# Feed forward accumulators over eight PSUM banks, and the modulation's sums over partitions later in the order

## The chip, the cores and the metric

One core of a Trainium2 chip runs the whole program. Its engines work side by side, each through its own list of instructions in a fixed order: TensorE (PE in the profile, with PEld for its weight loads), VectorE (DVE), ScalarE (ACT), GpSimd (POOL) and SyncE (SP), which here issues all DMAs. The metric is device time in microseconds of one execution. Matrix products accumulate in PSUM, which has eight banks; a tile of 128 x 512 f32 fills one bank.

## The reference, cut to what matters

Two transformer blocks on 1024 tokens of width 1024, all in f32. The part that the change touches is the feed forward at the end of the first block, and the modulation that opens the second:

```
u = causal_dwconv(h @ w_up, conv_w) + conv_b        # 1024 -> 2 x 2816 columns, 3 taps along the tokens
a, b = split(u, 2)
y = (silu(a) * b) @ w_down                           # 2816 -> 1024
h = h + rmsnorm(y, g5)

mod = silu(c) @ w_ada + b_ada                        # one row of 1024 times 1024 x 3072
shift, scale, gate = split(mod, 3)
h2 = rms_norm(h, g) * (1 + scale) + shift            # opens block 2; gate multiplies its output
```

## The kernel before, in words

The tokens are worked in two halves of 512. Each f32 operand is split into a high and a low part, so that one product is three matrix instructions (`mm3`, L178 to L180): high times high, high times low, low times high. A k tile of 128 rows of a weight comes as half of a 512 KB load into `raw`, is cut by ACT (high part `whi`, L143) and POOL (low part `wlo`, L144), and is used for four PSUM tiles, 12 instructions in all. `whi` and `wlo` have six buffers each, `raw` two.

PSUM's eight banks are divided by name. `A()` (L102) hands out tiles `pa` from four banks. `M()` (L105) hands out tiles `pm`: two banks without a name `ns`, and one bank each for `ns` 0 and 1. All large products of the feed forward use `A()`; transposes, the attention's small products and the modulation use `M()`.

`ffn` (L807) runs once per half, called FFN1 and FFN2 below. Its inner width of 2816 is 22 tiles of 128, in six groups: five of four tiles, and one of two. For one group, `up` (L814) makes two products of four PSUM tiles each, called up1 and up2 (96 instructions each; the last group has up1 alone). ACT copies each PSUM tile to `pad` (L817), DVE does the three taps of the convolution (L818 to L824), ACT the silu, DVE the product of the two halves (L829), and ACT and DVE split the result into `gh` and `gl`. Then `proj_R` makes the two halves of the output columns from the group before, called R0 and R1 (48 instructions each, 24 in the last group), and DVE adds each of their four PSUM tiles to `y` (L845 copies in the first group, L847 adds later). The order within the program is up1, up2, R0, R1 for each group. Since all four use the same four banks, each product begins when the readers of the one before have emptied them.

At the start of each `ffn` the other half of the tokens is still being normed. After `next(f)` has written up1 and up2 of the first group, `resid` adds the residual (L285 to L291) and `norm_T` (L294) norms the rows and transposes them over `pm` tiles (L223, eight tiles of four transposes) into the operand of the next stage, splitting each by ACT and DVE (L143, L144). The scheduler orders instructions by priority, so that this work of DVE stands between the convolutions of the first group. These two stretches, 1020 to 1080 us and 1440 to 1500 us, are called opening 1 and opening 2.

`mod` (L852) makes shift, scale and gate (j = 0, 1, 2). For each j, DVE multiplies eight blocks of `w_ada` by the column of silu(c) and adds them up in `mac` (L864, L866); each block is a 512 KB load into `wad`, of which there are two buffers. Then two products with a tile of ones sum `mac` over the partitions into `pm` tiles (L872, two passes each in the profile), DVE adds the bias (L873), and the row goes to DRAM (`mods`, L877), from where FFN2's opening reads scale and shift. `mod` is called in the opening of FFN1 with `high_priority(offset=-800)`, which lets its instructions be ordered later than their place in the code.

Of the kernel before, what the change touches and what calls it, by code (L numbers as in the profile page):

```python
# [9 lines left out]
F32 = mybir.dt.float32  # L10
# [7 lines left out]
P = 128  # L18
T = 1024
D = 1024  # L20
HT = 512
# [40 lines left out]
def weave(main, f, rate):  # L62
    """`rate` steps of f after each of main, then the rest of f"""
    due = 0.0
    for _ in main:
        due += rate
        while due >= 1:
            due -= 1
            next(f, None)
    run(f)  # L70


class Net:
    def __init__(self, tc, a, out):
        self.tc = tc
        self.nc = tc.nc
        self.a = a
        self.out = out

# [27 lines left out]

    def t(self, n, ns=""):
        return self.tp.tile([P, n], F32, name="tn", tag=f"tn{n}{ns}", bufs=8)
# [36 lines left out]
    # weights: src [pairs of k tiles, 128, 2, columns]  # L146
# [14 lines left out]
    def wplan(self, specs):  # L161
        """the units that wpair() hands out, in order"""
        self.wq = [src[i : i + 1] for src in specs for i in range(src.shape[0])]
        self.wready = []

    def wpair(self):
        """the next two k tiles, with the loads and splits of the following pairs under way"""
        while self.wq and len(self.wready) < LOOK:
            self.wready.append(self.wunits(self.wq.pop(0)))
        return self.wready.pop(0)  # L170
# [11 lines left out]
    # out[c, t]: 4 column tiles of 128, free = t  # L182
    def proj_T(self, units, xh, xl, nt=HT, ncol=4):
        ps = [self.A() for _ in range(ncol)]
        n = len(units)
        for k, (wh, wl) in enumerate(units):
            for c in range(ncol):
                s = slice(c * P, (c + 1) * P)
                self.mm3(ps[c][:, :nt], wh[:, s], wl[:, s], xh[:, k, :nt], xl[:, k, :nt], k == 0, k == n - 1)
        return ps  # L190

    # out[t, c]: t tiles of 128, free = columns
    def proj_R(self, units, xh, xl, ntt=NTT, nc=HT):
        ps = [self.A() for _ in range(ntt)]
        n = len(units)
        for k, (wh, wl) in enumerate(units):
            for t in range(ntt):
                s = slice(t * P, (t + 1) * P)
                self.mm3(ps[t][:, :nc], xh[:, k, s], xl[:, k, s], wh[:, :nc], wl[:, :nc], k == 0, k == n - 1)
        return ps  # L200
# [15 lines left out]
    # rows r [128, 1024] at t tile -> x hi/lo  # L216
# [12 lines left out]
    # rms norm of rows, times g, to x hi/lo  # L229
# [49 lines left out]
    def postnorm(self, y, g, hsrc, hdst):  # L279
        """y: two tiles [P, 4, 512]; y = hsrc + rms(y) g, also to hdst"""  # L280
        nc = self.nc
        r = self.sumsq_panels(y)
        for t in range(NTT):
            hr = self.R()
            nc.sync.dma_start(hr, hsrc[t * P : (t + 1) * P, :])  # L285
            for p in range(2):
                c = slice(p * HT, (p + 1) * HT)
                yt = y[p][:, t, :]
                nc.vector.scalar_tensor_tensor(yt, yt, r[:, t : t + 1], g[:, c], ALU.mult, ALU.mult)
                nc.vector.tensor_tensor(yt, yt, hr[:, c], ALU.add)  # L290
                nc.sync.dma_start(hdst[t * P : (t + 1) * P, c], yt)  # L291

    def norm_T(self, y, g, shift=None):
        """rms-normed rows of y (two panels), transposed"""  # L294
        nc = self.nc
        xh, xl = self.X(), self.X()
        r = self.sumsq_panels(y)
        for t in range(NTT):
            hr = self.R()
            for p in range(2):  # L300
                c = slice(p * HT, (p + 1) * HT)
                nc.vector.scalar_tensor_tensor(hr[:, c], y[p][:, t, :], r[:, t : t + 1], g[:, c], ALU.mult, ALU.mult)
                if shift is not None:
                    nc.vector.tensor_tensor(hr[:, c], hr[:, c], shift[:, c], ALU.add)
            self.rows_to_T([hr[:, :HT], hr[:, HT:]], xh, xl, t)
        return xh, xl
# [52 lines left out]
    def s1_qkv(self, u, xh, xl, qk, vv, gate):  # L359
        """q, k, v of the heads 2u, 2u + 1 after the short convolution, [d, t], and their gates, rows"""  # L360
# [22 lines left out]
        # the heads 0 and 1 bring the eight logits along  # L383
# [31 lines left out]
    def s1_specs(self):  # L415
        """the weights of stage 1 in the order of their use"""
        a = self.a
        first = [a["w_qk"][0], a["w_vga"][0], a["w_cfm"][0], a["w_qk"][1], a["w_vg"][0], a["w_cfm"][1]]
        second = [first[i] for i in (0, 1, 2, 5, 3, 4)]
        return first + second + 2 * [a["w_out"][0], a["w_out"][1]]  # L420

    def s1_ab(self, ab):
        """log decay and beta, [t, chunk, head]"""
# [37 lines left out]
    def s1_conv(self, j, xh, xl, cc):  # L461
        """gated and convolved conformer channels, [c, t]"""
# [52 lines left out]
    def gdn(self, u, qkv, dec, gate):  # L515
        """heads 2u, 2u + 1, 4 chunks of 128; multiplies the normed rows into `gate`"""
# [19 lines left out]
        # squares of q and k, summed over d  # L536
# [18 lines left out]
        def chunk(c):  # L555
# [19 lines left out]
            # decays  # L575
# [10 lines left out]
            # scores  # L586
# [8 lines left out]
            # (I + L)^-1 by doubling; U = -L^T, Xm the inverse within blocks, Y its transpose  # L595
# [30 lines left out]
            # the off-diagonal block of the two halves  # L626
# [18 lines left out]
            # scan  # L645
# [55 lines left out]
    # y = x @ w (rows), then the norms around the residual  # L701
# [41 lines left out]
    def xa_q(self, p, q, xh, xl):  # L743
        """queries of the heads 2p, 2p + 1"""
        units = self.wunits(self.a["xa_w_q"][p])
        ps = [self.A() for _ in range(4)]
        for k, (wh, wl) in enumerate(units):
            for c in range(4):
                s = slice(c * P, (c + 1) * P)
                self.mm3(ps[c], wh[:, s], wl[:, s], xh[:, k, :], xl[:, k, :], k == 0, k == NK - 1)  # L750
                yield
        for c in range(4):
            self.split(ps[c], q[0][:, 4 * p + c, :], q[1][:, 4 * p + c, :])
# [47 lines left out]
    def ffn(self, xh, xl, p3, fh):  # L801
# [6 lines left out]
        def up(kt, ng):  # L808
            gh = self.E(F32R)
            gl = p3.tile([P, 4, HT], F32R, name="gl", tag="gl", bufs=2)  # L810
            for j in range(0, ng, 2):
                ps = self.proj_T(self.wunits(wu[(kt + j) // 2]), xh, xl)
# [23 lines left out]
        for n, (kt, ng) in enumerate(groups):  # L836
# [3 lines left out]
            for p in range(2):  # L840
                units = self.wunits(wd[p, kt // 2 : (kt + ng) // 2])
                ps = self.proj_R(units, *g)
                for t in range(NTT):
                    if kt == 0:
                        v.tensor_copy(y[p][:, t, :], ps[t])  # L845
                    else:
                        v.tensor_tensor(y[p][:, t, :], y[p][:, t, :], ps[t], ALU.add)  # L847
# [4 lines left out]
    def mod(self, pm2):  # L852
# [5 lines left out]
        for j in range(3):  # L858
            ac = pm2.tile([P, D], F32, name="mac", tag="mac", bufs=1)
            for k in range(8):  # L860
# [4 lines left out]
                else:  # L865
                    v.scalar_tensor_tensor(ac, w, sc[:, k : k + 1], ac, ALU.mult, ALU.add)  # L866
            r = pm2.tile([P, D], F32, name="wad", tag="wad", bufs=2)
# [9 lines left out]
            nc.sync.dma_start(self.mods[j], r)  # L877

    def b2_open(self, ctx):
# [13 lines left out]
        # lower bounds  # L893
# [12 lines left out]
        # f = lb + (1 - lb) (tanh + 1) / 2  # L906
# [14 lines left out]
    def hgrn_head(self, i, qs, fe, vr, oA, ss):  # L921
        """qs, fe: silu(q) and tanh(f / 2), [d, t]; vr: [t, 4 tiles, 512] rows; head i"""
# [12 lines left out]
        # the two diagonal blocks of 64  # L935
# [43 lines left out]
        # rows of kG  # L979
# [6 lines left out]
        # states before the chunks 1..3 and after the last  # L986
# [21 lines left out]
    def gate_rows(self, zu, gu, xh, xl, gb, o, r):  # L1008
        """o [P, 4, 512] *= rstd[t, head] * silu(z) * sigmoid(g) * norm_g"""
# [16 lines left out]
    def rot(self, units, xh, xl, h, which):  # L1026
        """rows of 8 heads x 64, rotated, times the decay of the row -> [P, 4, 512]"""
# [21 lines left out]
    def ret_pair(self, i, qr, kr, vr, oB, ss):  # L1049
        """heads 2i, 2i+1"""  # L1050
# [159 lines left out]
    def final_proj(self, h, m, gate, fg):  # L1210
        """output projection and the final norm, row tile after row tile"""
# [36 lines left out]
    def run(self):  # L1248
# [3 lines left out]
        with ExitStack() as ctx:  # L1252
# [80 lines left out]
            with ExitStack() as c3:  # L1333
# [6 lines left out]
                xf = self.norm_T(y, gb(4))  # L1340
                with self.tc.high_priority(offset=-800):
                    self.mod(p3)
                *_, y = f
                f = self.ffn(*xf, p3, fh)
                next(f)
                self.resid(0, y, 2, 5)
                xb = self.norm_T(y, self.gbc(self.mods[1]), self.gbc(self.mods[0]))
                *_, y = f
            with ExitStack() as c4:
# [19 lines left out]
    def resid(self, h, y, s, gi):  # L1369
        """h_s = h_(s-1) + rms(y) g"""  # L1370
# [3 lines left out]
    def load_norm(self, src, g, ntt=NTT, shift=None, xs=None):  # L1374
        """rms-normed rows of src, transposed"""
# [8 lines left out]
def _host(inp):  # L1384
    """layout of the inputs and constants of the shapes"""
# [7 lines left out]
    # weights, a unit of columns after the other: [unit, pair of k tiles, 128, 2, columns]  # L1393
# [71 lines left out]
```

## Time and profile before

| what | value |
|---|---|
| median of 3 runs | 3004.94 us (3001.94 to 3011.28) |
| profiled execution, first to last instruction (its span) | 3007.8 us |
| TensorE busy in the profile | 2823.5 us, 94% |
| VectorE, GpSimd, ScalarE busy | 60%, 41%, 38% |
| feed forward, both halves | 1000.7 to 1823.8 us |

The profile gives no time of the profiled execution other than its span; it lies 2.9 us above the median of the timed runs. A matrix instruction is shown from its start to its modelled end, so that neighbours overlap: the pace is read from the distance of the starts. PEclk is the share of full clock that TensorE was granted; it has two levels, 1.0 (2.4 GHz) and 0.5 (1.2 GHz), and a fraction is a mean over a stretch.

### The profile page before, as it was taken

How to read it: one execution, taken by the hardware profiler on the slowest of the kernel's cores; microseconds unless marked ns; L12 is line 12 of the kernel's file. 1: busy time of each engine (PE TensorE's matmuls, PEld its weight loads, DVE VectorE, ACT ScalarE, POOL GpSimd, SP SyncE). 2: the span in 40 equal slices, each digit the busy share in tenths (PEclk: the TensorE clock that was granted, in tenths of full speed). 3: DMA queues.
4: the chain of work that ended last, by engine and by line, in shares of the span. 5: the costliest groups of instructions: out<-in, count | busy, mean ns of one | idle time of the engine just before them, and what ended most of it. 6: DMA issues, size and time to landing. Idle time of an engine off the chain costs nothing.

```text
span 3007.8 us, 41965 instructions
## 1 busy us (share of the span) xinstructions
PE 2823.5 (94%) x15828; PEld 2232.1 (74%) x15828; DVE 1813.9 (60%) x3605; ACT 1135.2 (38%) x2273; POOL 1234.5 (41%) x913
## 2 busy tenths in 40 slices
PE   7999898998999999899899999999999999999998
PEld 6676676777877777677677777787777777777776
DVE  6698889866345765743855556737545366464444
ACT  4443534455444433233433333232233333232333
POOL 3333323333342554354454544343443543434443
PEclk9999999999999999999999999999999999999999
DMA  4112111146242633622422225121323332222222
GB/s 152 50 64 64 50 45 55 36 133 192 68 140 86 202 99 100 208 91 84 130 91 91 85 91 170 51 88 56 96 74 97 99 119 71 82 63 83 85 75 101
DMA packets 136715, 287.07 MB, mean 95 GB/s; under 512 B 9792, under 2 KB 12736, under 8 KB 136512
## 3 DMA queue, kind: packets, MB, share of 16 engines
q1 hardware_dynamic: 136512, 284.38, 29.3%
q8 instruction: 125, 2.05, 0.3%
q14 instruction: 78, 0.64, 0.1%
HBM read 265.99 MB, written 18.35 MB: 95 GB/s over the span
## 4 chain that ended last, share of the span: by engine, by line
PE 49%; DVE 14%; ACT 2%; issue 2%; DMA 2%; POOL 1%; SPq 0%; ACTq 0%; DVEq 0%; POOLq 0%
PE pa L178 15%; PE pa L179 14%; PE pa L180 14%; DVE fo L824 3%; PE pm L944 2%; DVE fo L822 1%; POOL wlo L144 1%; DMA wad<-in_w_ada 1%; DVE fo L829 1%; DVE fh L819 1%; DVE pad L818 1%; DVE gl L144 1%; PE pm L1001 0%; PE pm L990 0%; PE pm L1000 0%
## 5 line engine op out<-in xcount | busy, mean ns | idle before, releaser
L144 POOL TENSOR_TENSOR wlo<-raw,whi 128x512 fp32r<-128x512 f32 (+1 forms) x792 | 1137.7, 1442 | 1668.7 <-ACT whi L143 1590.6
L143 ACT CAST whi<-raw 128x512 fp32r<-128x512 f32 (+1 forms) x808 | 496.7, 620 | 1131.3 <-PE pa L180 603.8
L178 PE MATMUL pa<-x,whi 128*128 128x512 f32 x1376 | 567.4, 413 | 18.8 <-ACT x L1130 10.3
L178 PE MATMUL pa<-whi,x 128*128 128x512 f32 (+2 forms) x1408 | 555.3, 396 | 12.4 <-ACT z L1015 3.8
L180 PE MATMUL pa<-x,wlo 128*128 128x512 f32 x1376 | 552.1, 401 | 0.1
L179 PE MATMUL pa<-x,whi 128*128 128x512 f32 x1376 | 551.9, 401 | 0.0
L180 PE MATMUL pa<-whi,x 128*128 128x512 f32 (+2 forms) x1408 | 547.5, 389 | 0.0
L179 PE MATMUL pa<-wlo,x 128*128 128x512 f32 (+2 forms) x1408 | 546.4, 388 | 0.0
L178 PEld LDWEIGHTS pa<-x,whi 128*128 128x128 f32 x1376 | 261.7, 190 | 82.1 <-ACT x L1130 11.2
L178 PEld LDWEIGHTS pa<-whi,x 128*128 128x128 f32 x1408 | 265.5, 189 | 75.6 <-issue 6.3
L180 PEld LDWEIGHTS pa<-x,wlo 128*128 128x128 f32 x1376 | 261.7, 190 | 62.5 <-issue 2.7
L180 PEld LDWEIGHTS pa<-whi,x 128*128 128x128 f32 x1408 | 265.5, 189 | 54.0 <-issue 0.9
L179 PEld LDWEIGHTS pa<-wlo,x 128*128 128x128 f32 x1408 | 265.6, 189 | 52.4 <-issue 1.2
L179 PEld LDWEIGHTS pa<-x,whi 128*128 128x128 f32 x1376 | 262.1, 190 | 54.2 <-issue 3.4
L480 DVE SCALAR_TENSOR_TENSOR e<-padc,cw,e 128x512 f32<-128x512 f32 x240 | 197.3, 852 | 1.2
L824 DVE SCALAR_TENSOR_TENSOR fo<-pad,cols,fo 128x512 f32<-128x512 f32 x176 | 168.5, 985 | 0.7
L178 PE MATMUL pa<-whi,e 128*128 128x512 f32 x352 | 143.3, 407 | 25.8 <-DVE e L847 20.4
L819 DVE COPY fh<-pad 128x2 f32<-128x2 f32 x88 | 27.3, 310 | 196.4 <-ACT pad L817 196.4
L179 PE MATMUL pa<-wlo,e 128*128 128x512 f32 x352 | 142.2, 404 | 0.0
L180 PE MATMUL pa<-whi,gl 128*128 128x512 f32 x352 | 141.9, 403 | 0.0
L144 DVE TENSOR_TENSOR x<-pm,x 128x512 fp32r<-128x512 f32 x112 | 75.0, 685 | 67.8 <-ACT x L143 67.3
L178 PEld LDWEIGHTS pa<-whi,e 128*128 128x128 f32 x352 | 68.0, 193 | 46.7 <-DVE e L847 23.9
(354 smaller groups left out, 3848.7 us busy)
## 6 DMA issues: line engine op xcount, KB each, us to landing
raw<-in_w_in SPq DMA_DIRECT2D x112, 512.0 KB, 3.7
raw<-in_ffn_w_up SPq DMA_DIRECT2D x88, 512.0 KB, 3.8
raw<-in_ffn_w_down SPq DMA_DIRECT2D x44, 512.0 KB, 4.0
raw<-in_w_out SPq DMA_DIRECT2D x32, 512.0 KB, 3.9
raw<-in_w_qf SPq DMA_DIRECT2D x32, 512.0 KB, 3.7
h<-e SPq DMA_DIRECT2D x48, 256.0 KB, 3.0
r<-h SPq DMA_DIRECT2D x24, 512.0 KB, 4.5
wad<-in_w_ada SPq DMA_DIRECT2D x24, 512.0 KB, 4.4
```

What stands on the lines that cost most here:

```text
L143: self.nc.scalar.copy(hi, src)
L144: (lo_eng or self.nc.vector).tensor_tensor(lo, src, hi.bitcast(F32), ALU.subtract)
L178: mm(ps, lhsT=lh, rhs=rh, start=first, stop=False)
L179: mm(ps, lhsT=lh, rhs=rl, start=False, stop=False)
L180: mm(ps, lhsT=ll, rhs=rh, start=False, stop=last)
L480: v.scalar_tensor_tensor(o, pad[:, k : k + HT], w(k), o, ALU.mult, ALU.add)
L818: v.tensor_copy(pad[:, :2], fh[:, i, :])
L819: v.tensor_copy(fh[:, i, :], pad[:, HT:])
L822: v.tensor_scalar(o, pad[:, 2:], self.col(k0 + 2), self.col(FB0 + i), ALU.mult, ALU.add)
L824: v.scalar_tensor_tensor(o, pad[:, k : k + HT], self.col(k0 + k), o, ALU.mult, ALU.add)
L829: v.tensor_tensor(ua, ua, ub, ALU.mult)
L944: mm(pm[64 * e : 64 * e + 64, c, :], lhsT=kG[:, s], rhs=q[:, s], start=True, stop=True)
```

## The change

A new function `banks` hands out four tiles of `A()` and four tiles of `M()` in turn, and the feed forward takes its accumulators from it. FFN1 calls it 23 times, so that FFN2's first product has the `pm` tiles. `mod` becomes a generator of four pieces: the sums of j = 0 and 1 in FFN1's opening, their products over the partitions and biases after FFN1, the sum of j = 2 in FFN2's opening, and its products after FFN2. `mac` gets a second buffer. The rest of the diff takes comments out, which moves line numbers (L178 to L180 are L184 to L186 in the changed kernel, L223 is L229, L866 is L873, L872 is L882).

```diff
+        self.turn = False
...
+    def banks(self):
+        self.turn = not self.turn
+        return [self.A() for _ in range(4)] if self.turn else [self.M(), self.M(), self.M(ns=0), self.M(ns=1)]
...
-    def proj_T(self, units, xh, xl, nt=HT, ncol=4):
-        ps = [self.A() for _ in range(ncol)]
+    def proj_T(self, units, xh, xl, nt=HT, ncol=4, ps=None):
+        ps = ps or [self.A() for _ in range(ncol)]
...
-                ps = self.proj_T(self.wunits(wu[(kt + j) // 2]), xh, xl)
+                ps = self.proj_T(self.wunits(wu[(kt + j) // 2]), xh, xl, ps=self.banks())
...
-                ps = self.proj_R(units, *g)
+                ps = self.proj_R(units, *g, ps=self.banks())
...
-        for j in range(3):
-            ac = pm2.tile([P, D], F32, name="mac", tag="mac", bufs=1)
+        def sums(j):
+            ac = pm2.tile([P, D], F32, name="mac", tag="mac", bufs=2)
...
+            return ac
+
+        def over_partitions(j, ac):
             r = pm2.tile([P, D], F32, name="wad", tag="wad", bufs=2)
...
+        acs = sums(0), sums(1)
+        yield
+        for j, ac in enumerate(acs):
+            over_partitions(j, ac)
+        yield
+        ac = sums(2)
+        yield
+        over_partitions(2, ac)
...
+                mod = self.mod(p3)
                 with self.tc.high_priority(offset=-800):
-                    self.mod(p3)
+                    next(mod)
                 *_, y = f
+                next(mod)
                 f = self.ffn(*xf, p3, fh)
                 next(f)
+                with self.tc.high_priority(offset=-800):
+                    next(mod)
                 self.resid(0, y, 2, 5)
                 xb = self.norm_T(y, self.gbc(self.mods[1]), self.gbc(self.mods[0]))
                 *_, y = f
+                run(mod)
```

On TensorE, between R0 and R1 of FFN1's first group, the last instructions of R0's fourth tile and the first of R1 stand so before:

```order
L178 MATMUL pa_10525<-whi_10518,e8_9495 128x512
L179 MATMUL pa_10525<-wlo_10519,e8_9495 128x512
L180 MATMUL pa_10525<-whi_10518,gl_9496 128x512
L178 MATMUL pa_10598<-whi_10580,e8_9495 128x512
L179 MATMUL pa_10598<-wlo_10581,e8_9495 128x512
L180 MATMUL pa_10598<-whi_10580,gl_9496 128x512
```

and so in the changed kernel:

```order
L184 MATMUL pa_10470<-whi_10463,e8_9495 128x512
L185 MATMUL pa_10470<-wlo_10464,e8_9495 128x512
L186 MATMUL pa_10470<-whi_10463,gl_9496 128x512
L184 MATMUL pm_10543<-whi_10525,e8_9495 128x512
L185 MATMUL pm_10543<-wlo_10526,e8_9495 128x512
L186 MATMUL pm_10543<-whi_10525,gl_9496 128x512
```

The order is the same; R1 now writes `pm` tiles while R0's `pa` tiles are being read.

On VectorE, in opening 1, before, the last sum of j = 0 (`mac`), and then the start of the residual's norm (`tn` are tiny columns of the reciprocal square root):

```order
L866 SCALAR_TENSOR_TENSOR mac_10033<-wad_10055,sc_10031,mac_10033 128x1024
L276 TENSOR_TENSOR tn_9876<-tn_9859 128x4
L136 TENSOR_SCALAR tn_9878<-tn_9876 128x4
L126 TENSOR_SCALAR tn_9881<-tn_9878 128x4
L127 TENSOR_SCALAR tn_9880<-tn_9881 128x4
L129 TENSOR_TENSOR tn_9881<-tn_9880 128x4
L130 SCALAR_TENSOR_TENSOR tn_9881<-tn_9881,tn_9878 128x4
```

In the changed kernel the same place reads:

```order
L873 SCALAR_TENSOR_TENSOR mac_10033<-wad_10055,sc_10031,mac_10033 128x1024
L871 TENSOR_SCALAR mac_10058<-wad_10059,sc_10031 128x1024
L873 SCALAR_TENSOR_TENSOR mac_10058<-wad_10062,sc_10031,mac_10058 128x1024
L873 SCALAR_TENSOR_TENSOR mac_10058<-wad_10065,sc_10031,mac_10058 128x1024
L282 TENSOR_TENSOR tn_9876<-tn_9859 128x4
L142 TENSOR_SCALAR tn_9878<-tn_9876 128x4
L132 TENSOR_SCALAR tn_9881<-tn_9878 128x4
L133 TENSOR_SCALAR tn_9880<-tn_9881 128x4
L135 TENSOR_TENSOR tn_9881<-tn_9880 128x4
L873 SCALAR_TENSOR_TENSOR mac_10058<-wad_10068,sc_10031,mac_10058 128x1024
L136 SCALAR_TENSOR_TENSOR tn_9881<-tn_9881,tn_9878 128x4
```

Sums of j = 1 (`mac_10058`) have come in front of the norm and into it: three of the eight in front, two within the reciprocal square root, two behind the residual, one in front of the second norm.

On TensorE, in opening 2, before, the third and the fourth group of transposes (`pm_13108`, `pm_13115`) stand among matrix instructions of the next group's up1:

```order
L180 MATMUL pa_13202<-x16_9927,wlo_13175 128x512
L223 MATMUL pm_13108<-ident_86,r4_13103 128x128 x4
L178 MATMUL pa_13203<-x16_9927,whi_13174 128x512
L179 MATMUL pa_13203<-x16_9928,whi_13174 128x512
L180 MATMUL pa_13203<-x16_9927,wlo_13175 128x512
L178 MATMUL pa_13204<-x16_9927,whi_13174 128x512
L179 MATMUL pa_13204<-x16_9928,whi_13174 128x512
L180 MATMUL pa_13204<-x16_9927,wlo_13175 128x512
L178 MATMUL pa_13205<-x16_9927,whi_13174 128x512
L179 MATMUL pa_13205<-x16_9928,whi_13174 128x512
L180 MATMUL pa_13205<-x16_9927,wlo_13175 128x512
L223 MATMUL pm_13115<-ident_86,r4_13103 128x128 x4
```

In the changed kernel:

```order
L185 MATMUL pm_13196<-x16_9928,whi_13179 128x512
L229 MATMUL pm_13099<-ident_86,r4_13094 128x128 x4
L186 MATMUL pm_13196<-x16_9927,wlo_13180 128x512
L229 MATMUL pm_13106<-ident_86,r4_13094 128x128 x4
L229 MATMUL pm_13118<-ident_86,r4_13113 128x128 x4
L229 MATMUL pm_13125<-ident_86,r4_13113 128x128 x4
L229 MATMUL pm_13137<-ident_86,r4_13132 128x128 x4
L229 MATMUL pm_13144<-ident_86,r4_13132 128x128 x4
L184 MATMUL pm_13193<-x16_9927,whi_13155 128x512
```

Six of the eight groups of transposes now stand together, since this up1 has `pm` tiles: two of its four tiles (`pm_13195`, `pm_13196`, the banks of `ns` 0 and 1) run ahead, and the other two (`pm_13193`, `pm_13194`) get their banks from the transposes.

## Rows read from the trace of the kernel before

**Rows 1.** The page, its head: the span.

```profile
span 3007.8 us, 41965 instructions
```

**Rows 2.** Waits of PE, 1000 to 1824: who for whom, us in total, times, longest.

```profile
PE pa L178 <- DVE e L847: 20.4, 8, 2.7
PE pm L872 <- DVE mac L866: 10.4, 2, 5.7
...
PE pa L178 <- DVE e L845: 5.4, 2, 2.7
```

**Rows 3.** Windows, PE alone: stretch and length, busy (instructions), PEclk, DMA share, GB/s.

```profile
1020.00:1080.00 60.00, 51.95 (x229) 0.94 0.43 147
1080.00:1220.00 140.00, 134.58 (x570) 0.99 0.36 112
1220.00:1270.00 50.00, 39.60 (x147) 0.86 0.61 212
1270.00:1440.00 170.00, 162.78 (x687) 0.98 0.30 95
1440.00:1500.00 60.00, 50.55 (x215) 0.91 0.39 124
1500.00:1823.80 323.80, 310.58 (x1323) 0.99 0.29 91
```

**Rows 4.** Timeline of PE, FFN1: start, duration, instruction [idle before <-releaser].

```profile
1000.67 0.39 PE L178 MATMUL pa<-x,whi 128*128 128x512 f32 x1
...
1022.66 0.40 PE L180 MATMUL pa<-x,wlo 128*128 128x512 f32 x1
...
1188.13 0.50 PE L178 MATMUL pa<-whi,e 128*128 128x512 f32 x1 [2.69 <-DVE e L847]
```

**Rows 5.** Timeline of DVE in FFN1's first two groups.

```profile
1150.66 0.51 DVE L819 COPY fh<-pad 128x2 f32<-128x2 f32 x1 [20.00 <-ACT pad L817]
...
1187.40 2.47 DVE L847 TENSOR_TENSOR e<-e,pa 128x512 f32<-128x512 f32 x4
```

**Rows 6.** Timeline of PE, the modulation's products of j = 1.

```profile
1226.02 3.78 PE L872 MATMUL pm<-mac,ones 128*128 128x512 f32 x4 [4.69 <-DVE mac L866]
```

**Rows 7.** Tile `wad`: durations in ns (min/median/max), DVE's idle time, landing times.

```profile
L866 DVE SCALAR_TENSOR_TENSOR mac<-wad,sc,mac x21: 1271/1285/2317, 981.9 to 1259.2; 128x1024 f32<-128x1024 f32 x21
...
  DMA wad<-in_w_ada: 32.7, 15
...
DMA to landing us min/median/max: 2.7/4.2/6.4
```

**Rows 8.** Timeline of DVE, opening 1.

```profile
1007.06 0.16 DVE L276 TENSOR_TENSOR tn<-tn 128x4 f32<-128x4 f32 x1 [5.87 <-ACT junk L227]
...
1024.63 0.98 DVE L819 COPY fh<-pad 128x2 f32<-128x2 f32 x1 [1.63 <-ACT pad L817]
```

**Rows 9.** Timeline of PE, opening 1.

```profile
1024.65 0.50 PE L178 MATMUL pa<-x,whi 128*128 128x512 f32 x1 [1.59 <-ACT pad L817]
...
1048.88 1.29 PE L223 MATMUL pm<-ident,r 128*128 128x128 f32 x8 [1.70 <-DVE r L302]
...
1061.13 1.11 PE L223 MATMUL pm<-ident,r 128*128 128x128 f32 x4 [4.72 <-DVE x L144]
```

**Rows 10.** Timeline of PE, opening 2.

```profile
1448.60 0.80 PE L178 MATMUL pa<-x,whi 128*128 128x512 f32 x1 [3.95 <-ACT pad L817]
...
1471.83 1.03 PE L223 MATMUL pm<-ident,r 128*128 128x128 f32 x8
...
1484.40 1.11 PE L223 MATMUL pm<-ident,r 128*128 128x128 f32 x4 [5.28 <-DVE x L144]
```

**Rows 11.** Timeline of DVE, opening 2.

```profile
1466.74 2.46 DVE L302 SCALAR_TENSOR_TENSOR r<-e,tn,gb 128x512 f32<-128x512 f32 x2
...
1483.67 0.68 DVE L144 TENSOR_TENSOR x<-pm,x 128x512 fp32r<-128x512 f32 x1
...
1497.33 0.68 DVE L144 TENSOR_TENSOR x<-pm,x 128x512 fp32r<-128x512 f32 x1
```

More of the change, by code (lines that the diff above doesn't have):

```diff
@@ L190, in proj_T, with proj_R @@
         return ps
-    def proj_R(self, units, xh, xl, ntt=NTT, nc=HT):
-        ps = [self.A() for _ in range(ntt)]
+    def proj_R(self, units, xh, xl, ntt=NTT, nc=HT, ps=None):
+        ps = ps or [self.A() for _ in range(ntt)]
         n = len(units)
```

## The prediction

> **What bounds the kernel now.** I read the head of the page first: the span is 3007.8 us [rows 1]. TensorE is busy for most of it, so any time in which it does not run at its pace is lost. Its waits in the feed forward come next. Two kinds lead [rows 2]: 10 waits on the adds to `y` (20.4 + 5.4 = 25.8 us, 2.7 us at most), before a product into `pa`; and two waits on the sums in `mac` (10.4 us). Then the pace: up1 of FFN1 has 96 instructions, starting 1000.67 to 1022.66 [rows 4], 95 steps, 0.2315 us each. With it the windows [rows 3] give the loss of a stretch, clock included: its length less the count (one taken off for an edge) times the pace.
>
> - Groups of FFN1 up to the modulation: 140 - 565 x 0.2315 - four passes of the modulation (1.8) = 7.4 us.
> - The modulation, 1220 to 1270: 50 - 138 x 0.2315 - 8 passes. Four passes took 3.78 us [rows 6] where PEclk is partly at the half level (mean 0.86, [rows 3]); I take 0.45 each at full clock, an estimate, so 3.6 in all. Loss 14.5.
> - The rest of FFN1: 170 - 686 x 0.2315 = 11.2. FFN2 behind its opening: 323.8 - 1322 x 0.2315 = 17.8.
> - Opening 1: 32 of the instructions are transposes at about 0.11 us (eight took 1.03 with the tail of the last [rows 10]): 60 - 196 x 0.2315 - 3.5 = 11.1. Opening 2 likewise: 60 - 182 x 0.2315 - 3.5 = 14.4.
>
> The reader is to see in the wait before R1 [rows 4] that TensorE is ready, idles 2.69 us, and is released by an add to `y`; and on DVE [rows 5] that this add begins at 1187.40, only 0.7 us before. DVE was late because it still had the convolutions of up2 in its queue, not because it is short of time: a few rows earlier it idles 20.00 us.
>
> **The change part by part.** *A. Eight banks.* R1 no longer writes the banks that R0's adds read. The 10 waits go, and with them the half clock that follows some of them (PEclk 0.98 to 0.99 in these windows [rows 3]): 7.4 + 11.2 + 17.8 = 36.4 us. What is late next: the following up1 takes the banks of R0, so its adds must be done when R1 ends. R1's 48 instructions take 48 x 0.2315 = 11.1 us; the adds begin at most 2.7 us after R1 may now start, and take 2.5 [rows 5]. That leaves about 6 us, and up2 after it has 22 more. So nothing takes their place: -36.4. Bounds: 0, if the waits come back at another product, and -36.4.
>
> *B. The modulation's products move to the end of each FFN.* There `mac` has long been summed. The passes themselves are paid in both kernels. The 14.5 us of loss go; in return the products of j = 1 wait for the bias adds of j = 0 to free the two `pm` banks, and FFN2's first tiles for those of j = 1. Queued behind them on TensorE is FFN2's up1. I take the nearest row, one four-pass block against two adds, as 1.5 us in all; bounds 0 and 4.7, the wait that such a product has now [rows 6]. -13.0. On SP the two stores of `mods` now stand in front of FFN2's later weight loads and wait for those adds; six `whi` buffers hold 6 x 12 x 0.2315 = 16.7 us of work for TensorE, which covers it.
>
> *C. Opening 1.* Eight sums of j = 1 come into DVE's queue, up to 1.285 us each [rows 7], 10.3 in all. Three fit into the 5.87 us in which DVE now waits for ACT's squares [rows 8]; 1.63 more are idle before the pads. The others, and their loads (4.2 us to landing, two buffers [rows 7]), push the rows for the first transposes back by an estimated 5 us, from 1048.88 to 1053.9. TensorE arrives 2 us sooner, since up2 no longer waits 1.59 us for up1's pads [rows 9]. So the first wait grows from 2.1 to 9.1, the second (4.72, [rows 9]) stays, and the half clock behind a wait of 9 us costs about 2 more than now. 11.1 becomes 18: +7. Bounds: -2, if all eight hide, and +21, if every sum also waits its share of DVE's idle time on these loads (32.7 / 15 = 2.2 us [rows 7]: 8 x 3.5 = 28, less the 7.5 idle). I take the low part, for the order leaves each later sum its two buffers ahead.
>
> *D. Opening 2.* The wait of 3.95 us for pads [rows 10] goes, with its share of half clock about 6 us. But DVE gets the bias adds and sums of j = 2. Four sums and the adds come before the rows for the first transposes, some 5.5 us later than the scaling that starts at 1466.74 [rows 11]; TensorE, which now arrives at about 1469.7, waits some 5.5 us where it waits for nothing at 1471.83 [rows 10]. Two more sums come before the first split, now at 1483.67 [rows 11]: about 1492, and TensorE, with 36 instructions between, waits some 6. Then six groups of transposes stand together, each needing a bank that DVE must empty first; DVE now takes from 1483.67 to 1498.0 for these splits [rows 11], 14.3 us, in which TensorE has some 3 us to do: 11 us of wait, where now the products between the transposes fill that time. Half clock behind all this: 5. So 5.5 + 6 + 11 + 5 = 27.5 instead of 14.4: +13. Bounds: -6 (only the pads' wait goes) and +28, if the eight sums wait 2.2 us each as well (15 more, taking the half clock along).
>
> Here the trace has one more thing to weigh. Around the wait for 5.28 us the clock is part of the time at half: opening 2 has PEclk 0.91 [rows 3]. The Trainium skill (TensorE: Matmul & The Clock Gate, Part 4: PE-mode transpose) says that transposes do not count as activity for the full clock in the way that matmuls do. By it the six groups together would prolong the half clock, and D would be some 3 us dearer; I leave the 5 us as they are, since 24 transposes take only about 2.6.
>
> Sum: -36.4 - 13.0 + 7 + 13 = -29.4 us. On the profiled execution 3007.8 - 29.4 = 2978.4; on the median, which lies 2.9 lower, 2975.5.
>
> **The rivals.** *The openings lose no more than now.* DVE's idle time takes the sums, and the transposes wait as before: -36.4 - 13.0 - 1.6 - 3.95 = -55, 2950 us. For it: DVE is idle for long stretches. Against: TensorE waits for DVE at both sets of transposes today. *The openings cost about twice the estimate:* +40 instead of +20, 2995 us. For it: the splits depend on DVE, ACT and TensorE in turn, and I have added them up by hand.
>
> *The waits only move.* With eight banks, DVE's adds are as late as before, and the next product on the same set waits: A is 0, and the rest -13 + 20 = +7, 3012 us. For it is that DVE's total work is unchanged; against it, the 20 us of idle time before each group [rows 5]. The Trainium skill tells of such a case (TensorE: Matmul & The Clock Gate, HAM oscillation): in one matmul kernel PSUM double-buffering gave no further gain. There the wait was on loads; here the releaser is the PSUM reader itself, and the trace does not bear the rule out.
>
> *Slower: the sums wait for their loads in the middle of DVE's queue.* DVE's list is in order, so a sum whose `wad` has not landed stops the convolutions and splits behind it. At a full 4.2 us of landing for each of 16 sums and 1.285 us of work, that is 88 us, less about 10 of idle time; TensorE would wait for nearly all of it: -36.4 - 13.0 - 5.6 + 78 = +23, 3028 us. It decides from about 3 us of wait per sum on (16 x 4.3 - 10 = 59 against 55). For it: a sum has waited 2.2 us on average. Against: those sums stood back to back.
>
> **How the numbers follow.** A measurement here can tell 0.3% (9 us) from no change: below 2996 is faster, above 3014 slower. Forecast 2975.5: 0.62. Openings free, 2950: 0.16. Openings twice as dear, 2995: 0.13, on the edge, 0.08 of it faster. Waits only move: 0.05, same (3012). Slower rival: 0.04, of it 0.03 slower. Faster 0.62 + 0.16 + 0.08 + 0.04 (the parts of the two last in which the price is lower) = 0.90, same 0.07, slower 0.03. The likeliest case's own range is 2962 to 2988, its bounds for C and D taken half way; reaching to the free and the dear openings makes 2950 to 2995.
>
> **What would show it.** A: no wait of PE for an add to `y` (the new L853) in the feed forward; the windows between the openings at the pace of 0.2315 and PEclk 1.00. B: the modulation's passes (L882) in two blocks, at the ends of the FFNs, with waits below 2 us. C: the first transposes of FFN1 waiting about 9 us for the scaled rows. D: PE waiting for splits over some 12 to 15 us around six groups of transposes. Wrong would be: waits of a product on `pad` or `y` in the middle of a group (A); DVE idle for `in_w_ada` over more than 20 us within the openings (the slower rival); waits of PE for `wlo`, which would mean late weight loads.

## The result and the profile after

The changed kernel takes 2975.45 us (median of 4, 2971.04 to 2979.18), the kernel before, run beside it, 3004.1 us. The ratio is 0.9898, with an interval of 0.9883 to 0.9914: faster by 1.0%. The forecast was 2975.5.

The page's head and its busy times, against [rows 1]:

```profile
span 2969.3 us, 41958 instructions
...
PE 2810.1 (95%) x15828; PEld 2226.8 (75%) x15828; DVE 1808.3 (61%) x3605; ACT 1134.5 (38%) x2273; POOL 1241.1 (42%) x913
```

The engines do the same work as before; what went is waiting. TensorE's waits in the feed forward, 1000 to 1824 us, against [rows 2] (us in total, times, longest):

```profile
PE pm L229 <- DVE r L308: 10.3, 3, 9.2
PE pm L229 <- DVE r L310: 9.5, 5, 5.5
PE pm L229 <- DVE x L150: 8.5, 3, 4.6
```

That is all of it. No product waits for an add to `y`, none for `mac`. Only transposes (L229) wait: for scaled and shifted rows (`r`) and for splits (`x`). The windows, against [rows 3] (stretch and length, busy (instructions), PEclk, DMA share, GB/s):

```profile
1020.00:1080.00 60.00, 45.94 (x203) 0.91 0.47 162
1080.00:1220.00 140.00, 140.00 (x605) 1.00 0.29 96
1220.00:1270.00 50.00, 50.00 (x218) 1.00 0.28 95
...
1500.00:1800.00 300.00, 300.00 (x1292) 1.00 0.31 101
```

Between the openings TensorE is busy all the time at full clock, one instruction every 140 / 605 = 0.2314 us, where it lost 7.4 and 14.5 us before. The modulation's passes now stand in two blocks, at the ends of the two halves (start, duration, instruction):

```profile
1384.99 3.78 PE L882 MATMUL pm<-mac,ones 128*128 128x512 f32 x8
...
1781.85 1.88 PE L882 MATMUL pm<-mac,ones 128*128 128x512 f32 x4
```

Eight passes take what four took in [rows 6], without a wait.

Since the same window holds other work in another kernel, the kernels are compared from here on by stretches cut at the same matrix instructions: the first 288 of FFN1 (opening 1), its other 1296, the same two for FFN2, and the first 200 of block 2. A stretch's loss is its length less 0.2315 us for each of them; transposes (some 3.5 us in an opening) and the modulation's passes stay in the loss.

| loss, us | opening 1 | rest of FFN1 | opening 2 | rest of FFN2 | start of block 2 |
|---|---|---|---|---|---|
| before | 14.8 | 38.9 | 17.9 | 18.1 | 6.4 |
| changed | 20.6 | 4.3 | 25.8 | 1.8 | 11.3 |
| banks_alone | 14.8 | 57.6 | 23.3 | 0.5 | 6.0 |
| mod_alone | 21.3 | 26.2 | 20.5 | 24.0 | 10.8 |
| banks_mac2 | 23.0 | 39.0 | 23.2 | 0.5 | 4.4 |
| start_on_pa | 20.9 | 3.7 | 19.9 | 1.8 | 10.7 |
| sums_late | 13.9 | 4.3 | 21.4 | 2.5 | 5.0 |
| products2_early | 21.1 | 4.3 | 25.8 | 2.5 | 5.9 |
| late_and_pa | 13.8 | 4.2 | 16.7 | 2.2 | 5.1 |

From before to changed the five differences sum to -32.3 us (+5.8, -34.6, +7.9, -16.3, +4.9). The two profiled spans differ by 38.5: the other 6.2 us lie in stretches that the change doesn't touch (3.6 of them ahead of FFN1), and are the spread between two executions. The medians differ by 28.7, with 26 to 35 by the interval.

### The profile page after: what moved, and what is told of

Same layout as the page of the kernel before. It is cut to its first block, busy times and chain, and to the rows that moved or that the text cites. A ratio compares the mean times of both kernels' runs of the same rounds, so it can differ in the third digit from the quotient of the medians.

```text
span 2969.3 us, 41958 instructions
## 1 busy us (share of the span) xinstructions
PE 2810.1 (95%) x15828; PEld 2226.8 (75%) x15828; DVE 1808.3 (61%) x3605; ACT 1134.5 (38%) x2273; POOL 1241.1 (42%) x913
## 5 line engine op out<-in xcount | busy, mean ns | idle before, releaser
L184 PE MATMUL pa<-whi,x 128*128 128x512 f32 (+2 forms) x1408 | 555.2, 395 | 11.4 <-ACT z L1034 3.8
L186 PE MATMUL pa<-whi,x 128*128 128x512 f32 (+2 forms) x1408 | 547.2, 389 | 0.0
L184 PE MATMUL pa<-x,whi 128*128 128x512 f32 x1024 | 425.5, 416 | 16.0 <-ACT x L1149 13.1
L185 PE MATMUL pa<-x,whi 128*128 128x512 f32 x1024 | 411.4, 402 | 0.0
L186 PE MATMUL pa<-x,wlo 128*128 128x512 f32 x1024 | 410.6, 401 | 0.1
L184 PEld LDWEIGHTS pa<-whi,x 128*128 128x128 f32 x1408 | 265.1, 188 | 74.9 <-issue 6.3
L186 PEld LDWEIGHTS pa<-whi,x 128*128 128x128 f32 x1408 | 265.2, 188 | 53.8 <-issue 0.9
L184 PEld LDWEIGHTS pa<-x,whi 128*128 128x128 f32 x1024 | 194.5, 190 | 61.5 <-ACT x L1149 13.9
L186 PEld LDWEIGHTS pa<-x,wlo 128*128 128x128 f32 x1024 | 194.1, 190 | 45.0 <-issue 1.7
L185 PEld LDWEIGHTS pa<-x,whi 128*128 128x128 f32 x1024 | 194.6, 190 | 39.0 <-issue 3.4
L184 PE MATMUL pm<-x,whi 128*128 128x512 f32 x384 | 153.7, 401 | 0.0
L185 PE MATMUL pm<-x,whi 128*128 128x512 f32 x384 | 152.5, 397 | 0.0
L186 PE MATMUL pm<-x,wlo 128*128 128x512 f32 x384 | 152.3, 397 | 0.0
L149 ACT CAST x<-pm 128x512 fp32r<-128x512 f32 x112 | 64.3, 589 | 67.2 <-PE pm L229 39.5
```

The lines of the kernel that those rows point to most:

```text
L149: self.nc.scalar.copy(hi, src)
L184: mm(ps, lhsT=lh, rhs=rh, start=first, stop=False)
L185: mm(ps, lhsT=lh, rhs=rl, start=False, stop=False)
L186: mm(ps, lhsT=ll, rhs=rh, start=False, stop=last)
```

## The experiments

Times of a kernel before are those of the runs beside it: 3005.79 us for banks_alone, mod_alone, start_on_pa and sums_late, 3007.09 for banks_mac2, products2_early and late_and_pa. The losses in the table are from one profiled execution of each kernel.

**banks_alone: the banks, without the move of the modulation.** The edit is the diff above without `mod`; in it `banks()` feeds the feed forward, the three sums and products stay in one piece in FFN1, and `mac` keeps its single buffer.

> The kernel before with the eight banks in turn, the modulation as it was (all three sums and products within FFN1). The losses below are lengths of stretches cut at the same matrix instructions, less 0.2315 us for each of them; before they are 14.8 us for FFN1's first 288, 38.9 for its rest, 17.9 for FFN2's first 288, 18.1 for its rest, 6.4 for the first 200 of block 2, and in the changed kernel 20.6, 4.3, 25.8, 1.8 and 11.3. Theory (the terms of the prediction, the banks and the modulation independent of each other): no wait for an add to y; 13, 19, 19, 2 and 6 us, so about -37 us and 2967 us. That is as fast as the changed kernel or faster: its moved sums cost in the two openings and behind FFN2 (5.8 + 7.9 + 4.9 us) what the moved products bring. Rival (the products have to be moved for the banks to pay, since mid-group they hold two of the pm banks that the next product wants): new waits around the products, the rest of FFN1 above 30 us, 2985 us or more.

Measured: 3017.31 us, ratio 1.0038 (1.0026 to 1.005). Slower than before; the rival was right. The waits of TensorE from 1000 to 1860 us, the first two groups:

```profile
PE pm L878 <- DVE mac L872: 47.3, 2, 24.0
PE pm L229 <- DVE r L310: 9.6, 4, 5.3
```

And its timeline there:

```profile
1115.50 3.78 PE L878 MATMUL pm<-mac,ones 128*128 128x512 f32 x4 [23.29 <-DVE mac L872]
1143.27 3.78 PE L878 MATMUL pm<-mac,ones 128*128 128x512 f32 x4 [23.98 <-DVE mac L872]
```

No product waits for `y` any more, and the rest of FFN2 loses only 0.5 us. But the second group's up2 now wants the two `pm` banks that the modulation also uses. So all six products of the modulation (12 passes) are ordered together in front of the part of up2 that takes those banks, and TensorE, in order, stands until the sums of j = 1 and then of j = 2 are made. Before, they shared `pm` with no product of the feed forward and could stand far apart among products into `pa`.

**mod_alone: the modulation moved, all accumulators in `pa`.**

```diff
-        return [self.A() for _ in range(4)] if self.turn else [self.M(), self.M(), self.M(ns=0), self.M(ns=1)]
+        return [self.A() for _ in range(4)]
```

> The changed kernel with all accumulators of the feed forward in the four pa banks, as before: only the modulation is moved. Theory of the prediction (B -13, C +7, and of D what the sums bring, 5.5 + 6, without the cluster of transposes, since the first product of FFN2 has pa banks): near 3004 - 13 + 7 + 9 = 3007 us, so no gain, with 10 waits for adds to y of about 26 us. From the trace of the changed kernel, with 4.9 us more at the start of block 2: up to 3010. Rival (the move of the modulation is where the gain of the changed kernel comes from, because the products in the middle of FFN1 disturb more than their own waits): 2990 us or less.

Measured: 3012.77 us, ratio 1.0023 (1.0015 to 1.0032). No gain, as the theory said; 2 to 3 us above its upper figure of 3010. The adds to `y` are waited for as before (two of its groups of waits):

```profile
PE pa L184 <- DVE e L853: 21.8, 8, 2.9
...
PE pa L184 <- DVE e L851: 5.4, 2, 2.7
```

In the rest of FFN2 its waits are about as long as before (13.5 against 13.2 us), but it loses 24.0 us instead of 18.1: two of them are the passes that now stand there, and PEclk is 0.97 instead of 0.99.

Each half of the change alone is slower than before, by 11.5 and 7.0 us; both together are faster by 28.7. The rest of FFN1 shows how they need each other: -12.7 us by the move alone, +18.7 by the banks alone, -34.6 by both.

**banks_mac2: banks_alone with a second `mac`.** To see what those 24 us were.

```diff
-            ac = pm2.tile([P, D], F32, name="mac", tag="mac", bufs=1)
+            ac = pm2.tile([P, D], F32, name="mac", tag="mac", bufs=2)
```

> The kernel with the eight banks alone, which lost 57.6 us in the rest of FFN1, with one edit: a second buffer for mac. There the six passes of the modulation stood together within the second group's up2, and TensorE waited 23.3 and 24.0 us for the sums of j = 1 and j = 2: these could not begin until the products of the j before had read mac. Theory (the wait is the chain products - mac's buffer - loads - sums, walked twice while TensorE's list stands): with two buffers the sums of j = 1 need not wait, one of the two waits goes, the rest of FFN1 loses some 33 us; the sums of j = 1 come into opening 1, which loses 21 instead of 14.8: 3000 us. Rival (TensorE waits because the loads of wad are late behind weight loads, not for mac's buffer): both waits stay in sum, above 45 us in the rest of FFN1, 3017 us or more.

Measured: 3004.35 us, ratio 0.9992 (0.9982 to 1.0002). One of the two waits is gone (1080 to 1200 us):

```profile
PE pm L878 <- DVE mac L872: 26.0, 1, 26.0
PE pm L878 <- DVE wad L879: 3.0, 1, 3.0
```

So the wait was for `mac`'s buffer, and then for eight loads and sums, once per j. The rest of FFN1 loses 39.0 (33 were expected: 26.0 for the wait that is left, and 3.0 for bias adds that had been overlooked), opening 1 23.0 (21). In time the kernel is the same as before: even with the second `mac`, the banks gain nothing while the products stay in the middle.

**start_on_pa: FFN2's first product on `pa`.** One line at the start of `ffn`:

```diff
+        self.turn = False
```

> The changed kernel with the turn set back at the start of each half, so that FFN2's first product has the pa banks and the next the pm banks. The transposes of opening 2 then stand apart between products of the following up1, as in opening 1. Theory (the cluster of six groups costs, waiting for splits one after the other): FFN2's first 288 instructions lose 20 instead of 25.8 us, 2970 us. It has a price: the last R1 of FFN1 has pa banks as well, so FFN2's first product waits for its adds to y, 1 to 2 us (the modulation's passes stand between). Rival (the splits are late because DVE has sums and bias adds in front of them, the cluster is only where TensorE notices): 25 to 27 us, and the time of the changed kernel, 2975.

Measured: 2969.0 us, ratio 0.988 (0.9867 to 0.9893); opening 2 loses 19.9 instead of 25.8. The cluster does cost what the theory said. The transposes of the changed kernel in opening 2:

```profile
1438.99 1.97 PE L229 MATMUL pm<-ident,r 128*128 128x128 f32 x8 [5.48 <-DVE r L310]
...
1455.44 1.12 PE L229 MATMUL pm<-ident,r 128*128 128x128 f32 x4 [4.56 <-DVE x L150]
...
1457.24 1.11 PE L229 MATMUL pm<-ident,r 128*128 128x128 f32 x4 [0.26 <-DVE x L150]
1460.51 1.09 PE L229 MATMUL pm<-ident,r 128*128 128x128 f32 x4 [2.15 <-DVE r L310]
1462.44 1.09 PE L229 MATMUL pm<-ident,r 128*128 128x128 f32 x4 [0.84 <-DVE r L310]
1463.69 1.09 PE L229 MATMUL pm<-ident,r 128*128 128x128 f32 x4 [0.16 <-DVE r L310]
1465.62 1.08 PE L229 MATMUL pm<-ident,r 128*128 128x128 f32 x4 [0.84 <-DVE r L310]
...
1466.35 0.77 PE L184 MATMUL pm<-x,whi 128*128 128x512 f32 x1
```

and those of start_on_pa:

```profile
1439.81 1.08 PE L229 MATMUL pm<-ident,r 128*128 128x128 f32 x4 [4.94 <-ACT pad L824]
1441.12 1.05 PE L229 MATMUL pm<-ident,r 128*128 128x128 f32 x4
...
1457.20 1.12 PE L229 MATMUL pm<-ident,r 128*128 128x128 f32 x4 [6.68 <-DVE x L150]
1460.45 0.60 PE L229 MATMUL pm<-ident,r 128*128 128x128 f32 x4
...
1466.10 0.63 PE L229 MATMUL pm<-ident,r 128*128 128x128 f32 x4 [0.43 <-DVE r L310]
```

The five waits of the cluster (4.25 us) shrink to one of 0.43, because products fill the time between the groups. Four of the five ended with scaled and shifted rows (`r`) and one, 0.26 us, with a split, so the theory named the wrong wait. And the waits are the smaller part of the gain: the one in front of the cluster's first group grows from 4.56 to 6.68 us, so that opening 2 waits 12.0 us in all instead of 14.3. The other 3.6 of the 5.9 us go with the clock. The cluster's 1.09 us for four transposes are the half clock, 0.60 the full one: from 1455 to 1468 us PEclk is 0.50 in the changed kernel and 0.80 here. The feared wait for R1's adds did not come.

**sums_late: no sum in an opening.** The multiplier is made dependent on `y`'s first group, and the products of j = 2 come before FFN2's last two groups. The calls of `mod` move behind that first group and lose their `high_priority`; of the edit only the two lines that make the dependence are shown.

```diff
...
+            s2 = pm2.tile([P, 8], F32, name="sc2", tag="sc2", bufs=1)
+            v.scalar_tensor_tensor(s2, y[1][:, NTT - 1, 0:8], 0.0, sc, ALU.mult, ALU.add)
...
```

> The changed kernel with the sums taken out of the openings: the column of silu(c) that they multiply by is made from y of the first group (times zero, plus the column), so none can start before y's first copies; j = 0 and 1 fall into FFN1's later groups, j = 2 into FFN2's, where DVE idles some 20 us in a group; the products of j = 2 come before FFN2's last two groups. Theory (C and D are DVE's work and load waits in front of the scaled rows and the splits): FFN1's first 288 lose 8 to 14 us instead of 20.6, FFN2's 18 to 20 instead of 25.8, the start of block 2 6.5 instead of 11.3: together about -18 us, 2957 us. Rival 1 (the openings are bound by ACT's squares, the norm's chain and the splits, whatever DVE does beside them): losses there as in the changed kernel, only the 4.9 us at block 2 come back, 2970 us. Rival 2 (16 or 8 loads of 512 KB in the middle of an FFN hold up the weights' loads behind them in SP's queue): waits for wlo or whi, above 2975 us.

Measured: 2957.68 us, ratio 0.9847 (0.9834 to 0.986). The theory holds, in opening 2 not quite: opening 1 loses 13.9 instead of 20.6, opening 2 21.4 (18 to 20 were expected). The loads cost TensorE nothing, though DVE waited for them in the middle of its list (tile `wad`):

```profile
  DMA wad<-in_w_ada: 19.8, 9
```

Why the sums weighed on opening 1 is seen on ScalarE, in the changed kernel

```profile
1049.48 0.62 ACT L149 CAST whi<-raw 128x512 fp32r<-128x512 f32 x1 [5.47 <-DMA raw<-in_ffn_w_up]
1050.01 2.04 ACT L823 COPY pad<-pm 128x512 f32<-128x512 f32 x4
```

and with the late sums:

```profile
1041.83 0.62 ACT L149 CAST whi<-raw 128x512 fp32r<-128x512 f32 x1 [4.16 <-DMA raw<-in_ffn_w_up]
1042.36 2.04 ACT L823 COPY pad<-pm 128x512 f32<-128x512 f32 x4
```

The copies that free up2's `pm` banks stand behind a weight's cast that waits for its load, and moved with the sums by 7.7 us (7.2 counted from FFN1's start). So the first transposes of opening 1 had two things to wait for that came at the same time, the scaled rows and the banks.

**products2_early: only the products of j = 2 earlier.**

```diff
+            yield None
...
+                for _ in range(4):
+                    next(f)
+                run(mod)
                 *_, y = f
-                run(mod)
```

> The changed kernel with only the products, bias and store of j = 2 moved, from behind FFN2 to before its last two groups; the sums stay in the openings. Theory for the 4.9 us that block 2's start loses in the changed kernel and that was not in the prediction (the store of the third row waits for the bias adds, and what opens block 2 is given memory only after it): the first 200 instructions of block 2 lose 5 to 7 us instead of 11.3, the openings stay at 20.6 and 25.8, 2970 us. Rival (it is the weights of block 2 or ACT's squares that are late, whatever the modulation does): 10 to 12 us, 2975 us.

Measured: 2971.82 us, ratio 0.9875 (0.986 to 0.9889). The start of block 2 loses 5.9 us instead of 11.3, the openings are unchanged (21.1, 25.8). By the time alone it can't be told from the changed kernel, since the intervals overlap; the stretch tells it. In the changed kernel, VectorE's timeline at the start of block 2:

```profile
1789.86 0.62 DVE L908 CAST hmask<-r 128x448 uint8<-128x448 f32 x1 [5.41 <-DMA mods<-wad]
```

TensorE's, where it waits next:

```profile
1835.53 0.79 PE L184 MATMUL pa<-x,whi 128*128 128x512 f32 x1 [7.33 <-ACT x L1149]
```

The first tile of block 2 waits for the store of the third row of `mods`, and 46 us later TensorE waits 7.33 us for an operand; with the products earlier that wait, in the grouped waits, is 2.2:

```profile
PE pa L184 <- ACT x L1150: 2.2, 1, 2.2
```

**late_and_pa: sums_late and start_on_pa in one.**

> The two edits that helped in one kernel: sums out of the openings, products of j = 2 before FFN2's last two groups, and the turn set back so that FFN2 starts on pa. Theory (late sums brought 17.9 us against the changed kernel, in opening 1 6.7, in opening 2 4.4, at block 2 6.3; starting on pa brought 5.9 in opening 2; both act on opening 2 by different waits, DVE's order and the cluster): FFN1's first 288 lose 14 us, FFN2's 15 to 16, the start of block 2 5: 2952 us. Rival (in opening 2 both remove the same wait, for the splits): FFN2's first 288 lose 19 to 21, 2957 us as with the late sums alone.

Measured: 2953.34 us (2950.67 to 2955.69), ratio 0.9814 (0.9799 to 0.9829), the fastest of all: 1.9% below the kernel before, 22 us below the changed one (medians of different occasions). Opening 2 loses 16.7, near the 15 to 16 of the theory, so DVE's order and the cluster are two costs, not one. Of TensorE's waits in opening 2, 1380 to 1480 us, two are left:

```profile
PE pm L229 <- DVE x L150: 4.6, 1, 4.6
PE pm L229 <- DVE r L310: 4.4, 1, 4.4
```

## Why the prediction was right, and where it was not

**A, the banks: right in size, wrong as a term by itself.** The waits for `y` went and nothing took their place: with B it predicted 49.4 us, and the two rests gave 34.6 + 16.3 = 50.9. What is left there is about the modulation's passes alone (3.78 and 1.88 us of 4.3 and 1.8). But the sum treated A and B as independent, and banks_alone shows that A without B costs 11.5 us; with the second `mac` it neither costs nor gains (3004 us in banks_mac2). The prediction looked for what is late next on `pa`; what it did not ask is who else uses the four banks that were added. The Trainium skill (Perfetto Trace Analysis, Matmul Optimizations and Matmuls) says to use all eight PSUM banks and to rotate independent groups through them so that reading one overlaps the next group. The rows agree, for kernels whose other users of those banks are out of the way: 2975 with them moved, 3017 with them left.

**B, the products at the ends: right.** No wait of 4.69 us or any other at either block; the 1.5 us allowed for the return were not needed. Missed was what comes next: behind FFN2 stands not more feed forward but the start of block 2, and its tiles wait for the store. That is the +4.9 us which no term had, shown by products2_early.

**C, opening 1: right.** +5.8 against +7. The first transposes waited 9.16 us (9.1 forecast), the second 3.67 (4.72):

```profile
1050.94 1.09 PE L229 MATMUL pm<-ident,r 128*128 128x128 f32 x4 [9.16 <-DVE r L308]
...
1064.26 0.66 PE L229 MATMUL pm<-ident,r 128*128 128x128 f32 x4 [3.67 <-DVE x L150]
```

The growth is all waiting, 8.0 us in the stretch before and 14.1 now; the 2 us more of half clock did not come. mod_alone, with +6.5, shows that it is all the sums. It also shows that the cause given, the scaled rows, is enough: its transposes share no bank with copies of up2, and its opening 1 loses as much. In the changed kernel the copies behind a weight load came as late as the rows, so either would have held the transposes. The low part of the bounds was the right choice: DVE's idle time for `in_w_ada` is 23.0 us in 9 waits (32.7 in 15 in [rows 7]). The last of them ends at 1003.86 us, before the window of opening 1, and opening 2 has none.

**D, opening 2: the direction right, the size and part of the mechanism not.** +7.9 instead of +13. The waits of 5.5 and 6 us measured 5.48 and 4.56. The failing step is "11 us of wait" for the cluster, which measured 4.25, and only 0.26 of it for splits: the other 3.99 us were waits for the rows that VectorE scales and shifts between its splits. The step set 14.3 us of VectorE's list, from 1483.67 to 1498.0 [rows 11], against 3 us of work for TensorE. The 14.3 us held seven splits, much other work and a wait of 1.54 us; the first seven splits now take from 1454.71 to 1466.12, 11.4 us. The six groups stand from 1455.44 to 1466.35, 10.9 us, and TensorE's own part of that is 6.7 us at the half clock, not 3. So a part of the half clock lay within the time that the step called waiting. In all of opening 2, the loss of 25.8 us less 14.3 of waits and 3.5 of transposes leaves 8.0 for the clock and whatever else is slow, where the prediction had 5. The prediction weighed 3 us more for the six groups of transposes and left them out; the runs don't tell whether the clock stayed low for the transposes or for the waits between them.

Two numbers of the prediction do not come out of its own working, and nothing hangs on them: the 2.1 us for the first wait before is a distance of starts, where the row has 1.70 [rows 9], and bounds taken half way give 2990 and not 2988.

The hit to 0.1 us is therefore partly luck: D was 5.1 us too dear, block 2's 4.9 us were missing, and the five stretches sum to -32.3 us where the medians differ by 28.7. Of the rivals, "the openings cost nothing", "about twice the estimate" (+13.7 us against +40) and "the waits only move" are out by the table. The slower rival, sums waiting for their loads in DVE's list, did not come about in the openings, as the waits for `in_w_ada` show. In the middle of the feed forward such waits cost nothing either: sums_late had 19.8 us of them, and TensorE none from them.

## What to carry to other kernels

When more banks are handed to a product, list who used them before and where those instructions can now stand in TensorE's order: one small product that waits for a late operand stops everything behind it, and the gain turns into a loss. Put work that only fills a sum where the filling engine idles and nobody waits; where a scheduler pulls it forward into any idle slot, a false dependence on a later result holds it back. Where a stage ends, ask what the next stage's first tile waits for.

## What the runs showed of the hardware

VectorE's smallest operations are not always small. In opening 1 of the changed kernel, on 128x4 elements,

```profile
1044.38 1.22 DVE L282 TENSOR_TENSOR tn<-tn 128x4 f32<-128x4 f32 x1
1045.62 1.19 DVE L142 TENSOR_SCALAR tn<-tn 128x4 f32<-128x4 f32 x1
1046.85 1.18 DVE L132 TENSOR_SCALAR tn<-tn 128x4 int32<-128x4 int32 x1
1048.07 0.17 DVE L133 TENSOR_SCALAR tn<-tn 128x4 int32<-128x4 int32 x1
```

while GpSimd had

```profile
1039.15 8.86 POOL L150 TENSOR_TENSOR wlo<-raw,whi 128x512 fp32r<-128x512 f32 x4 [3.73 <-ACT whi L149]
```

which ends at 1048.01: from then on the same kind of operation takes 0.17 us. The four splits in that row take 4.22, 2.24, 1.26 and 1.26 us, against a mean of 1.45 on the page, and each of the three slow operations ends 0.02 to 0.03 us after one of them (1045.57, 1046.79 and 1048.01). The Trainium skill (SBUF — State Buffer, SBUF: two separate sides) says that VectorE and GpSimd share one pair of ports, and that whichever of them takes it first holds it for a whole instruction. These rows agree. The kernel before and sums_late show the same three slow operations, so these make no difference between the kernels. The first split may make one: it takes 4.22 us here and 2.22 in the kernel before and in sums_late. The second split ends at 1045.57, and the next load of `raw` is issued at 1045.60; so some 2 us of the late cast in front of the copies of opening 1 would come from there, an estimate from the difference of the two durations.
